# Down projections that add the residual x late and load their weights first, and a first half step whose tokens all load at once

## The chip, the cores and the metric

The kernel runs on one core of one Trainium2 chip, in float32 with float32r matmul operands. The metric is the device time of one execution in microseconds (us), lower is better. The time of a kernel is the median of several executions; the profile shows one execution, with a time of its own.

The engines have short names throughout: PE is TensorE (matmuls), PEld its weight loads, DVE is VectorE, ACT is ScalarE, POOL is GpSimd, SP is SyncE, which here only issues DMA transfers. ACT issues DMA transfers too (ACTq rows), in the same in-order queue as its computing instructions.

## The reference, cut to what matters

One layer of a streaming encoder. 1024 prompt tokens and 8 x 16 sample tokens (together 1152 tokens, nine tiles of 128) go through two SwiGLU half steps around a mixer:

```python
def _swiglu(x, w_gate, w_up, w_down):
    return (jax.nn.silu(x @ w_gate) * (x @ w_up)) @ w_down

x = x + 0.5 * _swiglu(_rms_norm(x, norm_ff1), w_ff1_gate, w_ff1_up, w_ff1_down)
h = _rms_norm(x, norm_mix); proj = h @ w_in
# RWKV-7 scan on one part of proj, chunk-band attention (with a bias table) on the rest
x = x + concat(rwkv_out, att) @ w_out
x = x + 0.5 * _swiglu(_rms_norm(x, norm_ff2), w_ff2_gate, w_ff2_up, w_ff2_down)
y = _rms_norm(x, norm_final)
```

D_MODEL is 1024 and D_FF 2816. The change touches only the two half steps and the making of the attention bias tables, which is spread through the first down projection.

## The kernel before, in words

**Precision.** Every float32 matmul operand is split into a float32r high part (an ACT copy) and a low part (a subtraction on POOL or DVE); a product is three matmuls: high by high, high by low, low by high.

**Half step, first stage (gate and up).** The tokens are held in two parts (640 and 512 tokens). Each part is normed, transposed on PE and turned into seven "forms", sums and differences of quarter blocks for a seven-product block scheme: three in a tile FX (tag F3) and four in FT (tag F4). `_x_forms` makes them, one of four column chunks c at a time: transposes (L251), copies and splits (L261, L262), differences (L263), the ACT copy of FT (L269) and its low parts (L271 on DVE, L272 on POOL). `_w_forms` loads a 1 MB weight block into a `raw` tile and yields its seven forms (`frm` tiles, seven buffers; combinations in `cmb`, L297). `_gate_up` runs blocks m = 0 to 10: seven products t for either part p, gate, then up, and writes the hidden block to DRAM (`hd`, `he`). In block 0 of the first half step the order of products is set by `k.lead`: the first part's first three products, then the rest.

At the start of the kernel five tiles of tokens load, then a second norm loop loads four more into the same seven `frm` buffers that the weight forms use; it is written between the making and the running of part 0's form generator.

**Half step, second stage (`_down`).** Eleven blocks m of two hidden rows of 128. For each block the hidden values `hr` (1.1 MB) are read back and split into `h` (L431 on ACT, L432 on POOL), and two weight rows `raw` (0.5 MB each) are read and split into `spl` (L162 on ACT, L163 on POOL). Then for nine token tiles and two column halves, six matmuls (L449 to L451) fill one PSUM bank (eight banks rotate), and DVE adds it to x (L453). In block 0 the nine x tiles are loaded beside it (L423). In the last block each x tile is handed on (`done`): to the norm of the mixer in the first half step, to the final norm and the output in the second.

**Beside the first down projection** `_bias_tables` runs as a generator, one step per block from block 1 on: vectors, then a small table, then for each of four head pairs a row broadcast, a skewed copy through DRAM, 12 transfers in all, a few DVE operations and a write. Its transfers are all on ACT's queue, each waiting for the one before.

**What sets the order.** The framework does not keep each engine's program order. It runs the program through its own cost model and gives every engine and DMA queue, at each moment of that model, the earliest-written instruction that is ready; the order found there is then fixed, and on the chip each queue runs it strictly in order, waiting at its head. So an instruction written late can stand early in its queue if the model found it ready, and the model's idea of a transfer's length decides it. Memory follows the same rule: pools lie on a left and a right stack, and a tile of a new pool waits for the tiles that lay there before.

Of the kernel before, what the change touches and what calls it, by code (L numbers as in the profile page):

```python
# [9 lines left out]
F32 = mybir.dt.float32  # L10
# [10 lines left out]
NT = 9  # L21
# [90 lines left out]
def _bias_tables(k, a):  # L112

    nc = k.nc
    _more_vectors(k, a)
    yield
    room = k.xgp.tile([P, KC * TG], F32, tag="xg", bufs=6, name="room")
    tab = room[:8, 0:257]  # L120
    nc.scalar.dma_start(tab, a["rel_bias"][0])
    ext = room[:8, 384:768]
    nc.gpsimd.memset(ext, 0.0)
    nc.vector.tensor_scalar(ext[:, 127:384], tab, tab[:, 0:1], None, ALU.subtract)
    extd = k.tc.dram_tile([8, 384], F32, name="ext_d")
    nc.scalar.dma_start(extd, ext)
    k.maskb = room[:, 768:768 + P].rearrange("p (b q) -> p b q", q=NQ)
    nc.gpsimd.memset(k.maskb, 0.0)
    for step, base in ((-1, 0), (1, NQ - 1)):
        nc.gpsimd.affine_select(  # L130
            out=k.maskb, in_=k.maskb, pattern=[[step * NQ, NB], [0, NQ]], compare_op=ALU.is_ge,
            fill=NEG, base=base, channel_multiplier=-step)
    for p in range(NPAIR):
        yield
        buf = k.xgp.tile([P, KC * TG], F32, tag="xg", bufs=6, name="bias")
        rows = buf[:, 0:768]
        near = buf[:, 768:1280].rearrange("p (h c) -> p h c", h=2)
        samp = buf[:, 1280:1792].rearrange("p (h c) -> p h c", h=2)
        new = buf[:, 1792:1792 + 288].rearrange("p (h c) -> p h c", h=2)
        nc.scalar.dma_start(  # L140
            rows, extd[2 * p:2 * p + 2].rearrange("h c -> (h c)")[None, :].to_broadcast([P, 768]))
        sk = k.tc.dram_tile([P, 768], F32, name=f"skew{p}")
        nc.scalar.dma_start(sk, rows)

        nc.scalar.dma_start(near, bass.AP(sk.tensor, sk.offset + 127, [[767, P], [384, 2], [1, 256]]))
        for b in range(NB):
            nc.scalar.dma_start(new[b * NQ:(b + 1) * NQ],
                                bass.AP(sk.tensor, sk.offset + 127, [[767, NQ], [384, 2], [1, 144]]))
        nc.vector.memset(near[0:64, :, 192:256], NEG)
        for h in range(2):  # L150
            nc.vector.tensor_copy(samp[:, h, 0:P], new[:, h, 0:P])
            nc.vector.tensor_tensor(
                samp[:, h, P:].rearrange("p (b q) -> p b q", q=NQ),
                new[:, h, None, P:P + NQ].to_broadcast([P, NB, NQ]), k.maskb, ALU.add)
        k.bias[p] = k.tc.dram_tile([P, 4, 256], F32, name=f"bias{p}")
        nc.scalar.dma_start(k.bias[p].rearrange("p h c -> p (h c)"), buf[:, 768:1792])
# [8 lines left out]

def _load_w(k, src, shape, rearr, **kw):

    raw = k.w.tile([P] + shape, F32, tag="raw", bufs=k.nraw, name="raw")
    k.wq.dma_start(raw, src.rearrange(rearr, **kw) if rearr else src)
    pool, nspl = k.spl  # L170
    d = pool.tile([P, 2] + shape, F32R, tag="spl", bufs=nspl, name="spl")
    _split(k, d, raw)
    return d
# [6 lines left out]
def _rms(k, x, junk):  # L180

    nc = k.nc
    ss = k.sm.tile([P, 1], F32, tag="ss", name="ss")
    rs = k.sm.tile([P, 1], F32, tag="rs", name="rs")
    nc.scalar.activation(junk, x, AF.Square, accum_out=ss)
    nc.vector.tensor_scalar(rs, ss, 1.0 / DM, 1e-5, ALU.mult, ALU.add)
    nc.gpsimd.tensor_tensor(ss, rs, k.mhalf[:, 0:1], ALU.pow)
    return ss
# [87 lines left out]
def _form_tile(pool, part, forms):  # L276
    return pool.tile([P, 2, forms, 4, PARTS[part][1]], F32R, tag=f"F{forms}", bufs=1, name="F")
# [30 lines left out]
    yield form(a22), 6, "a"  # L308


def _gate_up(k, wg, wu, hd, m, between=None):

    nc = k.nc
    hs = [k.hx.tile([P, 2, 2, n], F32, tag=f"hs{p}", bufs=1, name="hs") for p, (o, n) in enumerate(PARTS)]
    for up, w in enumerate((wg, wu)):
        source = _w_forms(k, w[:, 2 * m * P:2 * m * P + 2 * P])
        forms = [] if m == 0 and not up else list(source)
        state = [{}, {}]
        turns = [(t, p) for t in range(7) for p in range(2)]
        if m == 0 or (up and m == NF // 2 - 1):  # L320
# [78 lines left out]
def _down_w(k, wd, f):  # L399
    raw = k.w.tile([P, DM], F32, tag="raw", bufs=k.nraw, name="raw")  # L400
    k.nc.sync.dma_start(raw, wd[f * P:(f + 1) * P, :])
    pool, n = k.dspl[f % len(k.dspl)]
    d = pool.tile([P, 2, DM], F32R, tag="spl", bufs=n, name="spl")
    _split(k, d, raw)
    return d


def _down(k, s, pool, wd, hd, xd, done, beside=(), then=None):

    nc = k.nc  # L410
    mm = nc.tensor.matmul
    beside = iter(beside)
    k.hp = hp = [pool(s, "ha")]
    k.h = hp[0]
    if len(k.dspl) == 1:
        k.dspl.append((pool(s, "wb"), 2))
    hp.append(pool(s, "hb"))
    k.xp = pool(s, "xb")
    k.psum, k.ptag, k.pbufs = pool(s, "psum_b", space=PSUM), "g", 8

    def x_load(i):
        k.x.append(k.xp.tile([P, DM], F32, tag=f"x{i}", bufs=1, name="x"))
        nc.sync.dma_start(k.x[i], xd[i])  # L423

    k.x = []
    for m in range(NF // 2):
        raw = hp[0].tile([P, 2, T], F32, tag="hr", bufs=1, name="hr")
        nc.sync.dma_start(raw, hd[m])
        h = hp[m % 2].tile([P, 2, 2, T], F32R, tag="h", bufs=1, name="h")
        for f in range(2):  # L430
            nc.scalar.activation(h[:, 0, f], raw[:, f], AF.Copy)  # L431
            nc.gpsimd.tensor_tensor(h[:, 1, f], raw[:, f], h[:, 0, f].bitcast(F32), ALU.subtract)  # L432
        d = [_down_w(k, wd, f) for f in (2 * m, 2 * m + 1)]
        if m == 0:
            for i in range(2):
                x_load(i)
        if m:
            next(beside, None)
        if m == NF // 2 - 1 and then is not None:
            then()  # L440
        for i in range(NT):
            if m == 0 and i + 2 < NT:
                x_load(i + 2)
            a = slice(i * P, (i + 1) * P)
            for n in range(2):
                b = slice(512 * n, 512 * n + 512)
                ps = _bank(k, "pd")
                for f in range(2):
                    mm(ps, h[:, 0, f, a], d[f][:, 0, b], start=f == 0, stop=False)  # L449
                    mm(ps, h[:, 0, f, a], d[f][:, 1, b], start=False, stop=False)  # L450
                    mm(ps, h[:, 1, f, a], d[f][:, 0, b], start=False, stop=f == 1)  # L451
                xs = k.x[i][:, b]
                nc.vector.tensor_tensor(xs, ps, xs, ALU.add)  # L453
            if m == NF // 2 - 1:
                done(i)

# [815 lines left out]
def tile_encoder_step(ctx: ExitStack, tc: tile.TileContext, *aps):  # L1272
# [4 lines left out]
    k = _K()  # L1277
    k.nc, k.tc, k.o, k.dq, k.wq, k.aq = nc, tc, o, nc.sync, nc.sync, nc.scalar
    k.qd, k.kd, k.qs, k.bias = {}, {}, {}, {}
    k.nraw, k.nspl, k.nt, k.nu = 2, 4, 20, 7  # L1280

    def pool(stack, name, side="left", **kw):
        kw.setdefault("bufs", 1)
# [2 lines left out]
    def x_rows(i):  # L1286
        return a["x_prompt"][0, i * P:(i + 1) * P, :] if i < NPT else a["x_sample"].rearrange("b t d -> (b t) d")
# [20 lines left out]
    with ExitStack() as s_rw, ExitStack() as s_xg:  # L1308
# [3 lines left out]
        with ExitStack() as sr, ExitStack() as s:  # L1312
            k.F = [(_form_tile(pool(sr, "fx", "right"), 0, 3), _form_tile(pool(s, "ft"), 0, 4))]
            f1 = pool(s, "f1")
            k.F.append((_form_tile(f1, 1, 3), _form_tile(f1, 1, 4)))
            k.ny, k.nyb = 4 * PARTS[0][1], 3
            k.hx = pool(s, "hx")
            k.w = pool(s, "wa")
            k.bsp, k.bst, k.nbs, k.bsw = k.hx, "y", 3, k.ny
            k.lead = 3  # L1320
            _gate_up_banks(k, s, pool)
            _constants(k, a)
            gain = _gain(k, a["norm_ff1"][0], k.hx, "hs1")

            def norm_part(p):
                xns = []
                for i in (range(5), range(5, 9))[p]:
                    x = k.w.tile([P, DM], F32, tag="frm", bufs=7, name="xn")
                    nc.sync.dma_start(x, x_rows(i))
                    junk = k.hx.tile([P, 4 * 320], F32, tag="hs0", bufs=1, name="junk")  # L1330
                    rs = _rms(k, x, junk[:, :DM])
                    nc.vector.scalar_tensor_tensor(x, x, rs, gain, ALU.mult, ALU.mult)
                    xns.append(x)
                return xns

            xns = norm_part(0)
            part = _x_forms(k, 0, xns)
            xns = norm_part(1)
            for _ in part:
                pass  # L1340
            for m in range(NF // 2):
                _gate_up(k, w[0], w[1], hd, m, lambda: [None for _ in _x_forms(k, 1, xns)])
        k.w = pool(s_xg, "w2", "right")
        k.nraw, k.spl = 2, (k.w, 3)
        k.dspl = [k.spl]
# [180 lines left out]
```

## Time and profile before

| | |
|---|---|
| time of before, median of 3 runs | 2612.99 us (2608.03 to 12799.39) |
| the profiled execution: its own time | 2605.25 us |
| its span, first to last instruction | 2603.5 us |
| mean granted TensorE clock | 0.962 |
| PE busy | 2422.6 us, 93% |
| DVE, ACT, POOL busy | 1124.8, 899.8, 1076.5 us |
| DMA | 284.75 MB, mean 109 GB/s |

Between the span and the profiled execution's own time lie 1.75 us. A row of a timeline gives the start in us from the span's start, the busy time in us of the merged instructions, engine, line of the code, operation, output and inputs, shapes, count, and in brackets the idle time of the engine before it with what ended it. The granted clock is a share of full speed: 1.00 is 2.4 GHz and 0.50 is 1.2 GHz.

The stages of the half steps in this execution: start and first gate/up stage 0 to 575 us, first down projection 575 to 882, second gate/up stage up to 2311, second down projection from there to the end.

### The profile page before, as it was taken

To read this page: it belongs to the slowest core of one execution; us is meant where nothing else is said; L and a number is where in the kernel's file an instruction comes from. 1 tells how busy PE (TensorE), PEld (TensorE's weight loads), DVE (VectorE), ACT (ScalarE), POOL (GpSimd) and SP (SyncE) were. 2 spreads that over 40 slices of the span, in tenths; PEclk is the share of its full clock that TensorE was granted. 3 is DMA by queue.
4 is the path that set the end of the run, shared out by engine and by line. 5 is a ranking of instruction groups with operands and counts; after the bars stand their busy time and mean duration, and the time that the engine had idled before them with its cause. 6 is when DMAs were issued, how large, how long until landed. Compare 5 with 4: busy or idle time off the path is not lost.

```text
span 2603.5 us, 43481 instructions
## 1 busy us (share of the span) xinstructions
PE 2422.6 (93%) x17415; PEld 2161.5 (83%) x17415; DVE 1124.8 (43%) x2346; ACT 899.8 (35%) x1903; POOL 1076.5 (41%) x966
## 2 busy tenths in 40 slices
PE   4999999988999999999997999897999999989998
PEld 3899999986888799899874666676999999988886
DVE  6322222214544533856854666346222222225555
ACT  5333333321111443443323576524333333321112
POOL 4545454444433233443213443105554544544332
PEclk8999999999999999999996899998999999999999
DMA  3222112227322324543658994522221122252221
GB/s 113 67 68 86 56 63 86 67 83 269 113 77 70 107 63 133 168 132 104 190 148 197 219 206 112 175 91 65 67 86 57 62 86 68 69 197 102 77 102 73
DMA packets 230283, 284.75 MB, mean 109 GB/s; under 512 B 54920, under 2 KB 183552, under 8 KB 227264
## 3 DMA queue, kind: packets, MB, share of 16 engines
q1 hardware_dynamic: 194044, 226.72, 27.8%
q0 software_dynamic: 7648, 25.43, 4.1%
q10 hardware_dynamic: 28388, 29.81, 3.5%
q8 instruction: 137, 2.24, 0.4%
q14 instruction: 66, 0.54, 0.1%
HBM read 191.79 MB, written 90.12 MB: 108 GB/s over the span
## 4 chain that ended last, share of the span: by engine, by line
PE 42%; DVE 5%; POOL 3%; issue 3%; ACT 2%; DMA 2%; ACTq 0%; POOLq 0%; DVEq 0%
PE pa L341 3%; PE pd L450 3%; PE pd L451 3%; PE pd L449 3%; PE pa L343 3%; PE pa L342 3%; PE pb L341 2%; PE pb L342 2%; PE pb L343 2%; POOL frm L292 2%; PE ps_s L1132 1%; PE ps_o L1186 1%; PE ps_pt L1171 1%; PE ps_yc L975 1%; PE ps_wo L1261 1%
## 5 line engine op out<-in xcount | busy, mean ns | idle before, releaser
L341 PE MATMUL pa<-F,frm 128*128 128x256 f32 (+1 forms) x1408 | 424.6, 302 | 34.7 <-ACT r L348 25.2
L343 PE MATMUL pa<-F,frm 128*128 128x256 f32 (+1 forms) x1408 | 419.3, 298 | 2.7 <-POOL frm L292 2.7
L342 PE MATMUL pa<-F,frm 128*128 128x256 f32 (+1 forms) x1408 | 419.3, 298 | 2.1 <-POOL F L272 2.1
L453 DVE TENSOR_TENSOR x<-pd,x 128x512 f32<-128x512 f32 x396 | 270.0, 690 | 243.1 <-PE pd L451 228.8
L163 POOL TENSOR_TENSOR spl<-raw,spl 128x1024 fp32r<-128x1024 f32 x78 | 187.6, 2408 | 453.0 <-ACT spl L162 453.0
L449 PE MATMUL pd<-spl,h 128*128 128x512 f32 x792 | 314.0, 397 | 14.8 <-ACT spl L162 12.1
L450 PE MATMUL pd<-spl,h 128*128 128x512 f32 x792 | 311.9, 394 | 13.3 <-POOL spl L163 13.3
L292 POOL TENSOR_TENSOR frm<-cmb,frm 128x512 fp32r<-128x512 f32 x176 | 230.1, 1309 | 221.7 <-ACT frm L291 221.3
L343 PE MATMUL pb<-F,frm 128*128 128x320 f32 (+1 forms) x1056 | 312.7, 296 | 3.1 <-POOL frm L292 3.1
L342 PE MATMUL pb<-F,frm 128*128 128x320 f32 (+1 forms) x1056 | 312.2, 296 | 3.1 <-DVE F L271 3.1
L341 PE MATMUL pb<-F,frm 128*128 128x320 f32 (+1 forms) x1056 | 313.3, 297 | 1.2 <-ACT frm L291 1.2
L451 PE MATMUL pd<-spl,h 128*128 128x512 f32 x792 | 311.8, 394 | 0.0
L341 PEld LDWEIGHTS pa<-F,frm 128*128 128x128 f32 x1408 | 268.9, 191 | 44.4 <-ACT r L348 33.0
L343 PEld LDWEIGHTS pa<-F,frm 128*128 128x128 f32 x1408 | 269.1, 191 | 3.5 <-POOL frm L292 3.5
L342 PEld LDWEIGHTS pa<-F,frm 128*128 128x128 f32 x1408 | 269.4, 191 | 2.5 <-POOL F L272 2.5
L292 POOL TENSOR_TENSOR frm<-raw,frm 128x512 fp32r<-128x512 f32 x132 | 173.8, 1318 | 186.7 <-ACT frm L291 186.7
L162 ACT ACTIVATE spl<-raw 128x1024 fp32r<-128x1024 f32 x78 | 82.2, 1055 | 406.3 <-PE pd L451 342.7
L343 PEld LDWEIGHTS pb<-F,frm 128*128 128x128 f32 x1056 | 200.2, 190 | 3.8 <-POOL frm L292 3.8
L342 PEld LDWEIGHTS pb<-F,frm 128*128 128x128 f32 x1056 | 200.1, 190 | 3.3 <-DVE F L271 3.3
L341 PEld LDWEIGHTS pb<-F,frm 128*128 128x128 f32 x1056 | 200.0, 189 | 1.8 <-ACT frm L291 1.8
L449 PEld LDWEIGHTS pd<-spl,h 128*128 128x128 f32 x792 | 150.1, 190 | 48.5 <-ACT spl L162 12.3
L450 PEld LDWEIGHTS pd<-spl,h 128*128 128x128 f32 x792 | 150.1, 189 | 48.3 <-POOL spl L163 16.2
(259 smaller groups left out, 4572.7 us busy)
## 6 DMA issues: line engine op xcount, KB each, us to landing
raw<-in_w_ff_gate_dram SPq DMA_DIRECT2D x22, 1024.0 KB
raw<-in_w_ff_up_dram SPq DMA_DIRECT2D x22, 1024.0 KB
raw<-in_w_ff_down_dram SPq DMA_DIRECT2D x44, 512.0 KB
raw<-in_w_in_dram SPq DMA_DIRECT2D x26, 512.0 KB
hr<-hd SPq DMA_DIRECT2D x11, 1152.0 KB
hr<-he SPq DMA_DIRECT2D x11, 1152.0 KB
q<-qk POOLq DMA_DIRECT2D x24, 384.0 KB, 7.6
x<-xd SPq DMA_DIRECT2D x18, 512.0 KB
```

Of the source, the lines that this page charges most:

```text
L162: k.nc.scalar.activation(dst[:, 0], raw, AF.Copy)
L163: k.nc.gpsimd.tensor_tensor(dst[:, 1], raw, dst[:, 0].bitcast(F32), ALU.subtract)
L292: nc.gpsimd.tensor_tensor(d[:, 1], x, d[:, 0].bitcast(F32), ALU.subtract)
L341: nc.tensor.matmul(ps, frm[:, 0, c], F[:, 0, jj, c], start=new and c == 0, stop=False, **kw)
L342: nc.tensor.matmul(ps, frm[:, 0, c], F[:, 1, jj, c], start=False, stop=False, **kw)
L343: nc.tensor.matmul(ps, frm[:, 1, c], F[:, 0, jj, c], start=False, stop=c == 3, **kw)
L449: mm(ps, h[:, 0, f, a], d[f][:, 0, b], start=f == 0, stop=False)
L450: mm(ps, h[:, 0, f, a], d[f][:, 1, b], start=False, stop=False)
L451: mm(ps, h[:, 1, f, a], d[f][:, 0, b], start=False, stop=f == 1)
L453: nc.vector.tensor_tensor(xs, ps, xs, ALU.add)
L975: mm(py[s, hh % 2], wout[:, hh, L:], mov[:, hh], start=True, stop=True)
L1132: mm(ps, q.qs[i // 3][:, j, h, t:t + P], q.ks[h][:, c0:c0 + n], start=j == 0, stop=j == 1)
```

## The change

Four edits.

1. `_down` writes a block's two weight loads and splits ahead of its hidden load and split; in block 0 the low part of h is subtracted on DVE instead of POOL.
2. `_down` no longer loads x in block 0. There ACT copies the bank into the x tile; from block 1 to 9 one tile of x per block is loaded into a single buffer `xin` and added to its x tile by DVE (128x1024), written after the first token tile.
3. `_bias_tables` yields more often, and a step is taken at the fourth and the seventh token tile of each block from 1 on, instead of once ahead of the block.
4. The first half step loads token tiles 0 to 4 into a spare tile (`hold`, where part 1's F3 tile comes later), the first gate weights, then tiles 5 to 8 into two `frm` buffers and one `raw` buffer, instead of waiting for `frm` buffers; the first weight form is written ahead of the token forms, part 0's forms ahead of the second norms, and `k.lead` is 5 instead of 3. (`_load_w` is adapted to a wider `raw` tile, without another transfer.)

```diff
@@ _bias_tables
         for h in range(2):
+            yield
             nc.vector.tensor_copy(samp[:, h, 0:P], new[:, h, 0:P])
@@ _gate_up
-def _gate_up(k, wg, wu, hd, m, between=None):
+def _gate_up(k, wg, wu, hd, m, between=None, gates=None, lead=()):
-        source = _w_forms(k, w[:, 2 * m * P:2 * m * P + 2 * P])
-        forms = [] if m == 0 and not up else list(source)
+        source = gates if gates and not up else _w_forms(k, w[:, 2 * m * P:2 * m * P + 2 * P])
+        forms = list(lead) if m == 0 and not up else list(source)
@@ _down
-    def x_load(i):
-        k.x.append(k.xp.tile([P, DM], F32, tag=f"x{i}", bufs=1, name="x"))
-        nc.sync.dma_start(k.x[i], xd[i])
-
-    k.x = []
+    k.x = [k.xp.tile([P, DM], F32, tag=f"x{i}", bufs=1, name="x") for i in range(NT)]
     for m in range(NF // 2):
+        d = [_down_w(k, wd, f) for f in (2 * m, 2 * m + 1)]
         raw = hp[0].tile([P, 2, T], F32, tag="hr", bufs=1, name="hr")
         nc.sync.dma_start(raw, hd[m])
         h = hp[m % 2].tile([P, 2, 2, T], F32R, tag="h", bufs=1, name="h")
         for f in range(2):
             nc.scalar.activation(h[:, 0, f], raw[:, f], AF.Copy)
-            nc.gpsimd.tensor_tensor(h[:, 1, f], raw[:, f], h[:, 0, f].bitcast(F32), ALU.subtract)
-        d = [_down_w(k, wd, f) for f in (2 * m, 2 * m + 1)]
-        if m == 0:
-            for i in range(2):
-                x_load(i)
-        if m:
-            next(beside, None)
+            (nc.gpsimd if m else nc.vector).tensor_tensor(
+                h[:, 1, f], raw[:, f], h[:, 0, f].bitcast(F32), ALU.subtract)
+        if 1 <= m <= NT:
+            xin = k.xp.tile([P, DM], F32, tag="xin", bufs=1, name="xin")
+            nc.sync.dma_start(xin, xd[m - 1])
...
         for i in range(NT):
-            if m == 0 and i + 2 < NT:
-                x_load(i + 2)
+            if i == 1 and 1 <= m <= NT:
+                nc.vector.tensor_tensor(k.x[m - 1], k.x[m - 1], xin, ALU.add)
+            if m and i in (3, 6):
+                next(beside, None)
...
                 xs = k.x[i][:, b]
-                nc.vector.tensor_tensor(xs, ps, xs, ALU.add)
+                if m:
+                    nc.vector.tensor_tensor(xs, ps, xs, ALU.add)
+                else:
+                    nc.scalar.copy(xs, ps)
@@ tile_encoder_step, first half step
-            k.F.append((_form_tile(f1, 1, 3), _form_tile(f1, 1, 4)))
-            k.lead = 3
+            k.lead, k.raww = 5, 2 * DM
...
-            xns = norm_part(0)
-            part = _x_forms(k, 0, xns)
-            xns = norm_part(1)
-            for _ in part:
+            hold = f1.tile([P, 2 * 3 * 4 * PARTS[1][1]], F32, tag="F3", bufs=1, name="hold")
+            xns = [normed(i, hold[:, i * DM:(i + 1) * DM]) for i in range(5)]
+            gates = _w_forms(k, w[0][:, 0:2 * P])
+            lead = [next(gates)]
+            for _ in _x_forms(k, 0, xns):
                 pass
-            for m in range(NF // 2):
-                _gate_up(k, w[0], w[1], hd, m, lambda: [None for _ in _x_forms(k, 1, xns)])
+            rest = [k.w.tile([P, DM], F32, tag="frm", bufs=7, name="xn") for _ in range(2)]
+            two = k.w.tile([P, 2 * DM], F32, tag="raw", bufs=2, name="xn")
+            rest += [two[:, :DM], two[:, DM:]]
+            xns = [normed(5 + i, x) for i, x in enumerate(rest)]
+            k.F.append((_form_tile(f1, 1, 3), _form_tile(f1, 1, 4)))
+            _gate_up(k, w[0], w[1], hd, 0, lambda: [None for _ in _x_forms(k, 1, xns)], gates, lead)
+            for m in range(1, NF // 2):
+                _gate_up(k, w[0], w[1], hd, m)
+            k.raww = DM
```

`normed(i, x)` is the body of the old norm loop for one tile: load, square and sum on ACT (L185), 1/rms (L186, L187), scale on DVE (L1332).

## Rows read from the trace of the kernel before

**Rows 1.** Busy time by stretches of 20 us: for PE, PEld, DVE, ACT and POOL the busy us and the count, then granted clock, DMA share, GB/s.

```profile
40.00:60.00 20.00, 11.17 (x51) 8.93 (x52) 15.56 (x32) 9.06 (x20) 9.00 (x6) 0.72 0.00 1
60.00:80.00 20.00, 15.02 (x83) 14.15 (x83) 11.19 (x18) 10.36 (x19) 15.99 (x11) 0.77 0.17 52
580.00:600.00 20.00, 7.80 (x20) 5.29 (x21) 3.64 (x4) 4.22 (x4) 9.95 (x5) 0.54 0.87 329
620.00:640.00 20.00, 16.64 (x71) 12.60 (x70) 14.17 (x23) 6.35 (x6) 14.92 (x6) 1.00 0.67 223
660.00:680.00 20.00, 20.00 (x88) 16.28 (x87) 10.51 (x16) 4.12 (x4) 10.27 (x5) 1.00 0.33 118
2300.00:2320.00 20.00, 13.24 (x97) 12.11 (x96) 2.20 (x6) 5.38 (x7) 12.84 (x8) 0.88 0.67 228
```

**Rows 2.** Timeline of SP's DMA queue in the first gate/up stage: the token loads, and the writes of hidden blocks 1 and 2 (two transfers each).

```profile
0.81 3.77 SPq L1329 DMA_DIRECT2D xn<-in_x_prompt_dram  x7
29.68 0.34 SPq L1329 DMA_DIRECT2D xn<-in_x_prompt_dram  x1
...
159.12 1.18 SPq L377 DMA_DIRECT2D hd<-hs  x2
205.65 1.24 SPq L377 DMA_DIRECT2D hd<-hs  x2
```

**Rows 3.** Timelines of DVE and POOL in the first 75 us, put in order of time: differences of part 0 (L263, 128x320), the norm of token tile 7 (L1332), and the low parts of FT (L272; 128x960 is part 0, 128x768 part 1).

```profile
32.23 1.28 DVE L263 TENSOR_TENSOR bs<-ps_n,bs 128x320 f32<-128x320 f32 x3
36.10 2.25 POOL L272 TENSOR_TENSOR F<-bs,F 128x960 fp32r<-128x960 f32 x1
36.18 3.26 DVE L1332 SCALAR_TENSOR_TENSOR xn<-xn,ss,gain 128x1024 f32<-128x1024 f32 x1 [0.94 <-POOL ss L187]
41.83 0.88 DVE L263 TENSOR_TENSOR bs<-ps_n,bs 128x320 f32<-128x320 f32 x2
72.11 1.98 POOL L272 TENSOR_TENSOR F<-bs,F 128x768 fp32r<-128x768 f32 x1
```

**Rows 4.** What PE waited for from 575 to 900 us, the first down projection: us in total, times, longest.

```profile
PE pd L449 <- ACT spl L162: 12.1, 1, 12.1
PE pd L450 <- POOL spl L163: 6.5, 3, 4.4
...
PE pd L449 <- DVE x L453: 2.0, 2, 1.7
```

**Rows 5.** Timeline of SP's queue at the start of the first down projection, and of SP's waits from 560 to 660 us.

```profile
564.66 13.67 SPq L428 DMA_DIRECT2D hr<-hd  x2
578.43 0.86 SPq L401 DMA_DIRECT2D raw<-in_w_ff_down_dram  x2
579.38 24.60 SPq L423 DMA_DIRECT2D x<-in_x_prompt_dram  x8
...
611.82 0.80 SPq L401 DMA_DIRECT2D raw<-in_w_ff_down_dram  x2
...
SPq L401 <- DMA bias<-skew: 21.2, 4, 10.6
```

**Rows 6.** Timelines of PE, ACT, POOL and DVE at the start of the first down projection.

```profile
595.07 0.79 PE L450 MATMUL pd<-spl,h 128*128 128x512 f32 x1 [0.67 <-POOL spl L163]
...
583.90 2.22 ACT L431 ACTIVATE h<-hr 128x1152 fp32r<-128x1152 f32 x2 [10.90 <-DMA hr<-hd]
586.02 1.04 ACT L162 ACTIVATE spl<-raw 128x1024 fp32r<-128x1024 f32 x1
590.85 1.06 ACT L162 ACTIVATE spl<-raw 128x1024 fp32r<-128x1024 f32 x1 [3.79 <-DVE room L124]
615.54 1.06 ACT L162 ACTIVATE spl<-raw 128x1024 fp32r<-128x1024 f32 x1 [23.64 <-DMA raw<-in_w_ff_down_dram]
...
585.14 5.20 POOL L432 TENSOR_TENSOR h<-hr,h 128x1152 fp32r<-128x1152 f32 x2 [5.07 <-ACT h L431]
590.31 4.71 POOL L163 TENSOR_TENSOR spl<-raw,spl 128x1024 fp32r<-128x1024 f32 x2
```

**Rows 7.** Timelines of PE, ACT and POOL at the start of the second down projection.

```profile
2310.79 0.39 PE L449 MATMUL pd<-spl,h 128*128 128x512 f32 x1
2316.59 0.79 PE L450 MATMUL pd<-spl,h 128*128 128x512 f32 x1 [5.41 <-POOL spl L163]
2319.59 0.80 PE L450 MATMUL pd<-spl,h 128*128 128x512 f32 x1 [1.35 <-POOL spl L163]
2325.68 0.40 PE L449 MATMUL pd<-spl,h 128*128 128x512 f32 x1
...
2311.26 1.06 ACT L162 ACTIVATE spl<-raw 128x1024 fp32r<-128x1024 f32 x1 [1.02 <-DMA raw<-in_w_ff_down_dram]
...
2308.31 5.25 POOL L432 TENSOR_TENSOR h<-hr,h 128x1152 fp32r<-128x1152 f32 x2 [0.18 <-ACT h L431]
2314.21 2.33 POOL L163 TENSOR_TENSOR spl<-raw,spl 128x1024 fp32r<-128x1024 f32 x1
2317.19 2.34 POOL L163 TENSOR_TENSOR spl<-raw,spl 128x1024 fp32r<-128x1024 f32 x1
```

**Rows 8.** An ACT copy out of PSUM, and the steady pace of the down stage: an eviction on DVE with the wait for PE ahead of it.

```profile
566.32 0.39 ACT L348 ACTIVATE r<-pa 128x256 f32<-128x256 f32 x1 [8.18 <-PE pa L343]
...
2355.84 0.69 DVE L453 TENSOR_TENSOR x<-pd,x 128x512 f32<-128x512 f32 x1 [0.67 <-PE pd L451]
```

More of the change, by code (lines that the diff above doesn't have):

```diff
@@ L166, in _load_w @@
 def _load_w(k, src, shape, rearr, **kw):
-    raw = k.w.tile([P] + shape, F32, tag="raw", bufs=k.nraw, name="raw")
+    raw = k.w.tile([P, k.raww], F32, tag="raw", bufs=k.nraw, name="raw")[:, :DM]
+    if len(shape) == 2:
+        raw = raw.rearrange("p (a b) -> p a b", b=shape[1])
     k.wq.dma_start(raw, src.rearrange(rearr, **kw) if rearr else src)
@@ L1279, in tile_encoder_step @@
     k.qd, k.kd, k.qs, k.bias = {}, {}, {}, {}
-    k.nraw, k.nspl, k.nt, k.nu = 2, 4, 20, 7
+    k.nraw, k.raww, k.nspl, k.nt, k.nu = 2, DM, 4, 20, 7
     def pool(stack, name, side="left", **kw):
@@ L1323, in tile_encoder_step, with normed @@
             gain = _gain(k, a["norm_ff1"][0], k.hx, "hs1")
[L1325 to L1334, printed above, removed]
-            xns = norm_part(0)
-            part = _x_forms(k, 0, xns)
-            xns = norm_part(1)
-            for _ in part:
-                pass
-            for m in range(NF // 2):
-                _gate_up(k, w[0], w[1], hd, m, lambda: [None for _ in _x_forms(k, 1, xns)])
+            def normed(i, x):
+                nc.sync.dma_start(x, x_rows(i))
+                junk = k.hx.tile([P, 4 * 320], F32, tag="hs0", bufs=1, name="junk")
+                rs = _rms(k, x, junk[:, :DM])
+                nc.vector.scalar_tensor_tensor(x, x, rs, gain, ALU.mult, ALU.mult)
+                return x
+            hold = f1.tile([P, 2 * 3 * 4 * PARTS[1][1]], F32, tag="F3", bufs=1, name="hold")
[3 more added lines that the diff above has]
+            for _ in _x_forms(k, 0, xns):
+                pass
+            rest = [k.w.tile([P, DM], F32, tag="frm", bufs=7, name="xn") for _ in range(2)]
[7 more added lines that the diff above has]
+            k.raww = DM
         k.w = pool(s_xg, "w2", "right")
```

## The prediction, made before the changed kernel ran

> **What bounds the kernel now.** I read the busy time by stretches first, because it tells stages apart: in the steady part of a down projection PE is busy for 20.00 of 20 us at full clock, while at 40 to 80 us, 580 to 600 us and 2300 to 2320 us it is not, and the granted clock is down there as well, 0.54 in the lowest [rows 1]. So PE is the bound of the half steps, DVE, ACT and POOL have room there (10.5, 4.1 and 10.3 of 20 us), and only the three places where a stage begins can give time back. The middle of the kernel, between the two half steps, is not touched. Then I read what PE waited for and, in the timelines, what had made the releaser late.
>
> *The start.* Seven token tiles load at once, two more wait for `frm` buffers until 29.68 us [rows 2]. The norm of tile 7 then takes DVE at 36.18, ahead of the last differences of part 0: chunk 2 of four has them done at 33.5 (32.23 + 1.28), chunk 3 only at 42.7. Part 1's last low part is done at 74.1 (72.11 + 1.98) [rows 3]. Hidden blocks are written every 46.5 us (205.65 - 159.12), so block 0 ended about 46.5 us before 159.1, at 112.6: 38.5 us after the last form [rows 2, 3].
>
> *The first down projection.* PE waits 12.1 us for the first weight split, then three times for POOL's low parts, in all 6.5 us, and 2.0 us for evictions [rows 4]. Why the weights are late is in SP's queue: the weights of block 0 left at 578.43, behind the hidden load of block 1, which had to wait until POOL had read the buffer; eight x loads follow until 604, the ninth behind them, and the weights of block 1 leave only at 611.82, after waits for bias-table transfers of ACT's queue (21.2 us in four) [rows 5]. On POOL the low parts of block 1's h (585.14 to 590.34) stand ahead of block 0's weights (590.31 to 595.02), and ACT held the second weight for 3.79 us behind a bias-table step. PE runs without gaps from 595.07 [rows 6].
>
> *The second down projection.* PE waits 5.41 and 1.35 us for POOL, which does 5.25 us of h and then 2 x 2.33 us of weights; PE runs on from 2319.59, at half clock (matmuls of 0.8 us) until 2325.68, where they take 0.40 us [rows 7].
>
> **The change, part by part.**
>
> *Start.* Nine token tiles and 1 MB of gate weights now go out first, the up weights later. At the 329 GB/s of 580 to 600 us [rows 1] these 5.8 MB take 18 us, so all tokens should be there by about 20 us. DVE's work is the same too; what goes is its order. Without the norm of tiles 7 and 8 between chunks 2 and 3, chunk 3 follows chunk 2 by one chunk's DVE work, about 4 us (eight operations of around 0.47 us, from 0.88 for two and 1.28 for three [rows 3]): 37.5 instead of 42.7, 5 us. The norms of tiles 5 and 6, loaded with the first seven, stood ahead of part 0's forms and now stand behind: 2.5 us more. I carry 7.5 us through to part 1's last form, because DVE idles 4.4 and 8.8 us of the two stretches from 40 to 80 [rows 1] and can take the norms in. With five products instead of three run ahead of part 1, two products of part 0 move into time that was a wait: a product is 1/14 of a block's part-0 half, 46.5 x 320/576 / 14 = 1.8 us, so 3.5 us. Sum **-11 us**. Ends: -18 (DVE idles 13.2 us from 40 to 80, and all of it goes, with the 3.5 us), and +3 for the first weight form, which now stands ahead of the token forms on ACT: if its 1 MB lands late, ACT waits for it, and 1 MB at that rate, 3.2 us, is the price.
>
> *First down projection.* Written first does not mean issued first: the old program too had block 0's weights ahead of block 1's hidden load, and the queue has them the other way round [rows 5]. So I do not count on weights that arrive before PE needs them. What frees the queue is that the hidden buffer is read by DVE: 1152 elements at the pace of the 1.28 us norm of 1024 [rows 3] are 1.44 us against POOL's 2.6 (5.20 for two [rows 6]), so the weights leave some 3.5 us earlier, near 575; the first landed 7.6 us after issue (586.02 - 578.43), the rest of the chain is as before. PE runs on from about 591: -4. The x loads leave the queue, so block 1's weights can leave earlier; of the 3.4 us that block 1 cost PE (1.4 of the 6.5 and the 2.0 [rows 4]) I take back 2, since waits on ACT's transfers remain. ACT's evictions: a copy of 256 columns is 0.39 us and one of 1024 is 1.06, so 512 take 0.6 [rows 6, 8]; 18 of them, 11 us, lie beside PE's 18 x 1.36 = 24.5 us [rows 8]: nothing, as long as ACT isn't held for longer than eight banks cover, 10.9 us. The nine additions of `xin`, 1.28 us each and 3.26 at worst beside POOL [rows 3], fall on a DVE that is half idle: nothing; without that cover 11.5 us a down projection. The load of one tile per block has 24.5 us of time; the DVE addition that waits for it has the evictions of its block queued behind it, and PE behind those after eight banks. The later steps of the bias tables are needed only far behind, in attention. Sum **-6 us**; ends -21 (the 12.1, 6.5 and 2.0 all go) and +13 (second rival).
>
> *Second down projection.* POOL loses the 5.25 us of h. The second weight's split on ACT ends at 2312.3, its low part 2.33 us later, with one 0.7 us product of the stage before between: about 2315.4 instead of 2319.6, so -4.2. A rule about DVE and POOL takes part of it back. The norm of 36.18 that took 3.26 us ended 1.1 us after POOL's operation beside it (36.10 + 2.25 = 38.35; 39.44), just its own 1.28 us: the two did not run side by side [rows 3]. The two subtractions of 1.44 us on DVE may so hold POOL for up to 2.9 us; I take 1.2. The Trainium skill, page "SBUF — State Buffer", section "Who interferes with whom", says that a DVE instruction with two SBUF inputs and a GpSimd instruction that reads SBUF exclude each other for their whole length; this trace agrees, and by that rule alone the term would be -1.3 instead of -4.2. The clock: 14 matmuls run at half pace from 2319.59 to 2325.68, 6.1 us instead of 3.2 (1.36/6 each). The waits of 1.4 and 1.7 us in block 1 lie in 620 to 640 us, where the clock is 1.00 [rows 1, 4]; after the wait of 5.41 it was half [rows 7]. The new wait lies between; I take half of 2.9. Sum **-4.5 us**; ends -1 and -11 (5.4 + 1.4 + 2.9, and more than that isn't lost). The nine x loads ahead of the first evictions cost PE nothing there before.
>
> Sum -21.5 us on the profiled execution's own 2605.25 (its span is 2603.5): 2583.8. The lowest run shown is 2.8 above that execution, the median 7.7, with an outlier that lifts it; I add 2.8: **2586 us**, 1% below 2612.99. About 2%, 52 us, is what a measurement of this kernel can tell from no change.
>
> **The rivals.**
>
> *Weights in time.* The queue's order does change, weights go out while the last products still run, and PE passes from one stage to the next without its wait and without half clock. Against it: the old order [rows 5]; for it: the second down projection, where weights followed the hidden load at once. Price: -15, -21 and -11, so 2605.25 + 2.8 - 47 = 2561.
>
> *ACT holds the evictions (slower).* ACT waited 23.64 us for a weight of block 1 [rows 6], whose load waited for bias-table transfers that ACT itself issues. Before, nothing that PE needed at once stood behind; now block 0's evictions do. Eight banks cover 10.9 us; a wait of 23.6 costs 12.7. With one such wait the first down projection loses 12.7 instead of gaining 6, and the time is 2605. With one for either weight of the block it loses 25.4 against 15.5 gained elsewhere: 2618, slower than before. It decides from holds of 26.4 us together beyond the cover of the first. Against it: the x loads that made transfers slow are gone.
>
> *The order doesn't change.* The framework's model leaves the forms of the start and the queue of the first down projection nearly as they are, and only POOL's relief counts: -3, -3.5 and -3, so 2598.
>
> **How the numbers follow.** Forecast 0.50; order unchanged 0.20; weights in time 0.13; ACT holds once 0.10, twice 0.07. The range of 8 in 10 goes from 2561 to 2606: it leaves out the slower case and the better half of the best one, and some of each end. Faster by over 2% (below 2560.7) needs nearly all of the first rival's sum: 0.07. Slower by over 2% has no case here, I leave 0.02 for one I don't see. Within 2%: 0.91.
>
> **What would show it.** Right: part 1's last L272 ends near 66 instead of 74; block 1's hidden write stands some 11 us earlier; the first weight of the down projection leaves SP near 575 and PE is gapless from about 591 after the old stage end; at the second, PE's wait for POOL's weights is about 2 us and few matmuls take 0.8 us. Wrong: an ACT wait over 11 us in block 0 with PE waiting for ACT's copies; DVE waiting for `xin`; or a weight load issued before the last gate/up product, which makes it the first rival.

## The result, and the profile after

The changed kernel takes 2578.59 us, median of four runs (2576.16 to 2579.73), against 2611.04 us for the kernel before, median of four of which one is the outlier of 12799.39. The ratio of the means, without that outlier, is 0.9878, with a 95% interval from 0.9859 to 0.9898: 1.2% faster, clear of noise, though less than the 2% that the prediction took as the least one could tell. The forecast was 2586 us. The profiled execution has a span of 2578.0 us, 25.5 us less than before, where the sum of the terms had been 21.5. (The medians are 32.5 us apart because the profiled execution of the kernel before, 2605.25 us, was a quick one.)

The total was near; its terms were not. I cut each profiled execution at five places: the write of hidden block 1, the end of the last gate/up matmul, the start of the first down projection's last matmul, the end of the second gate/up stage, and the end of the span. The first column runs from the span's start to the first mark and each of the next four from one mark to the next, in us; "middle" is everything between the two down projections, which no kernel here edits.

| kernel | to block 1's write | to the end of gate/up | first down | middle | second down | span |
|---|---|---|---|---|---|---|
| before | 159.1 | 415.9 | 306.7 | 1429.3 | 292.6 | 2603.5 |
| after | 154.4 | 416.6 | 291.1 | 1430.1 | 285.7 | 2578.0 |
| e1 start only | 155.9 | 416.1 | 307.9 | 1430.6 | 291.7 | 2602.3 |
| e2 order only | 159.4 | 416.0 | 306.1 | 1432.7 | 289.7 | 2603.9 |
| e3 DVE low part only | 158.7 | 416.6 | 307.6 | 1432.6 | 288.6 | 2604.1 |
| e4 late x only | 159.3 | 416.1 | 305.0 | 1430.4 | 293.1 | 2603.9 |
| e5 DVE low part and late x | 161.2 | 416.7 | 296.9 | 1424.5 | 288.0 | 2587.2 |
| e6 after, old written order | 153.9 | 416.6 | 293.1 | 1433.2 | 289.4 | 2586.2 |
| e7 after, POOL low part | 155.9 | 415.9 | 302.8 | 1431.8 | 290.4 | 2596.8 |
| e8 after, early x | 156.0 | 416.8 | 309.3 | 1428.3 | 286.9 | 2597.3 |
| e9 after, old steps | 154.5 | 416.5 | 291.5 | 1430.6 | 285.0 | 2578.1 |
| e10 after, lead 3 | 150.2 | 416.4 | 290.1 | 1429.7 | 285.2 | 2571.6 |
| e11 after, FT on DVE | 152.8 | 416.9 | 290.3 | 1432.1 | 284.6 | 2576.8 |
| e12 both of these | 147.0 | 416.8 | 290.0 | 1434.7 | 285.0 | 2573.5 |

The middle says how far a single execution can be read: it spreads over 10 us. In e6 PE, ACT and DVE run it in the same order as in the changed kernel, and it is 3.1 us longer. Nine executions of the kernel before, beside e12, lie between 2603.48 and 2617.88. So I compare stages and what ended the waits in them, not single totals.

From before to after, rounded from hundredths: start -4.7, gate/up +0.8, first down -15.6, middle +0.9, second down -6.8.

By stretches of 20 us (PE, PEld, DVE, ACT, POOL busy and counts, then granted clock, DMA share, GB/s), answering [rows 1]:

```profile
40.00:60.00 20.00, 13.88 (x66) 11.12 (x66) 11.97 (x24) 9.11 (x21) 8.59 (x7) 0.76 0.01 2
60.00:80.00 20.00, 17.25 (x106) 16.07 (x106) 14.39 (x24) 10.08 (x20) 16.24 (x11) 0.78 0.33 106
580.00:600.00 20.00, 20.00 (x79) 16.08 (x79) 0.00 (x0) 11.59 (x18) 12.41 (x5) 0.89 0.64 223
2280.00:2300.00 20.00, 18.18 (x124) 16.35 (x124) 5.48 (x8) 8.94 (x12) 14.11 (x9) 1.00 0.78 257
```

From 580 to 600 us PE is now busy throughout, where it was busy for 7.80 us. What PE waited for from 555 to 900 us (us in total, times, longest), answering [rows 4]:

```profile
PE pd L449 <- ACT spl L163: 2.6, 1, 2.6
PE pd L450 <- POOL spl L164: 2.5, 2, 1.5
PE pa L344 <- DVE y L357: 0.8, 1, 0.8
```

And from 2270 us to the end, answering [rows 7]:

```profile
PE pd L451 <- DVE h L432: 1.3, 2, 0.7
PE pd L449 <- ACT h L431: 0.5, 1, 0.5
```

The 12.1, 6.5 and 2.0 us of the first down projection became 2.6, 2.5 and nothing; the 6.8 us of the second became 1.8. The reason stands in SP's queue, answering [rows 2, 5]:

```profile
154.41 1.18 SPq L380 DMA_DIRECT2D hd<-hs  x2
...
559.96 0.34 SPq L428 DMA_DIRECT2D hr<-hd  x1
568.21 0.82 SPq L404 DMA_DIRECT2D raw<-in_w_ff_down_dram  x2
571.37 0.33 SPq L428 DMA_DIRECT2D hr<-hd  x1
576.04 2.94 SPq L404 DMA_DIRECT2D raw<-in_w_ff_down_dram  x2
```

One of SP's waits there, from 555 to 660 us:

```profile
SPq L404 <- DMA vrows<-in_mu_shift_dram: 7.8, 1, 7.8
```

Block 0's weights now leave ahead of block 1's hidden load, 2.9 us before the gate/up stage ends (571.06), and block 1's at 576.04 instead of 611.82.

### The profile page after: what moved, and what is told of

It reads as the page before. It is cut to its first block, busy times and chain, and to the rows that moved or that the text cites. A ratio compares the mean times of both kernels' runs of the same rounds, so it can differ in the third digit from the quotient of the medians.

```text
span 2578.0 us, 43273 instructions
## 1 busy us (share of the span) xinstructions
PE 2421.8 (94%) x17415; PEld 2160.3 (84%) x17415; DVE 1127.8 (44%) x2332; ACT 918.4 (36%) x1939; POOL 1077.6 (42%) x962
## 4 chain that ended last, share of the span: by engine, by line
PE 73%; DVE 8%; POOL 5%; issue 5%; ACT 3%; DMA 3%; ACTq 0%; POOLq 0%; DVEq 0%; SPq 0%
PE pd L449 7%; PE pd L451 7%; PE pd L450 7%; PE pa L344 7%; PE pa L346 6%; PE pa L345 6%; PE pb L344 3%; PE pb L345 3%; PE pb L346 3%; POOL frm L295 3%; PE ps_p L229 2%; PE ps_p L230 2%; PE ps_p L231 2%; PE ps_s L1135 2%; PE ps_pt L1174 1%
## 5 line engine op out<-in xcount | busy, mean ns | idle before, releaser
L454 DVE TENSOR_TENSOR x<-pd,x 128x512 f32<-128x512 f32 x360 | 244.1, 688 | 201.8 <-PE pd L451 201.8
L294 ACT ACTIVATE frm<-cmb 128x512 fp32r<-128x512 f32 x176 | 110.3, 628 | 198.7 <-PE pa L346 121.5
L451 PEld LDWEIGHTS pd<-spl,h 128*128 128x128 f32 x792 | 149.4, 189 | 36.3 <-DVE h L432 2.2
```

What stands on the lines that cost most here:

```text
L294: nc.scalar.activation(d[:, 0], x, AF.Copy)
```

## The experiments

Each ran once with a profile, unless a number of runs is given.

**One part at a time, on the kernel before.** e1 takes the start alone (edit 4), e2 to e4 take one edit of `_down` each:

```diff
e2: the line  d = [_down_w(k, wd, f) ...]  moves ahead of the hidden load
e3: +  (nc.gpsimd if m else nc.vector).tensor_tensor(h[:, 1, f], ...)
e4: ACT evicts block 0, one xin per block from 1 on, no x loads in block 0
```

> The kernel before with the start edit alone (tokens at once, first weight form early, lead 5). The trace of the changed kernel writes hidden block 1 at 154.41 us instead of 159.12, and everything else it gains lies later. If the start edit stands by itself, this kernel writes block 1 near 154.4, the rest is as before, and the total is 4 to 6 us under before. If the start gained more and gave it back to the rest of the change, or the other way round, block 1 comes before 152 or after 157.

> The kernel before with only the written order changed: a block's weight loads ahead of its hidden load, the low part of h still on POOL. Theory A (the order in which the loads are written does not decide the queue; the engine of the low part does): in the first down projection block 1's hidden load still stands ahead of block 0's weights in SP's queue, PE's first wait there stays near 12 us and PE runs gapless some 20 us after the last gate/up product, as before; total within 4 us of before. Theory B (weights written first is what brought the 15 us): the weights leave before block 1's hidden load, the wait falls to about 3 us, total 8 us or more under before.

> The kernel before with only the low part of block 0's h moved from POOL to DVE in both down projections. Theory A: block 1's hidden load has to wait longer in the framework's model, so block 0's weights go out ahead of it; PE's first wait falls from 12.1 to 3 to 5 us, PE runs gapless 8 to 12 us earlier in the first down projection, and the second one gains 3 to 5 us; total 12 to 16 us under before. Theory B: only POOL's relief, 4 us and 3 us, total 5 to 8 us under before.

> The kernel before with only x late: no x loads in block 0, ACT copies the banks there, one tile of x per block after that; written order, POOL's low part and the steps of the bias tables as before. Theory A: block 0 starts as late as before (wait near 12 us), and only the 3.4 us that block 1 cost PE go; total 2 to 5 us under before. Theory C (the x loads crowded the transfers, so that weights were late): the first waits fall by 6 us or more, total 8 us or more under before. If ACT's bias-table waits hold the evictions, PE waits for ACT's copies and the total is over before.

Measured: 2604.01, 2605.61, 2605.85 and 2605.66 us, against 2604.07 for the kernel before. No part alone gains anything in total, where 4 to 6 us were expected of e1, 12 to 16 (or 5 to 8) of e3 and 2 to 5 of e4. In the stages, e1 gains 3.2 us at the start. e2 leaves the first down projection as it was, with the weights behind both hidden loads (theory A), and takes 2.9 us off the second. e3 does move the weights ahead of block 1's hidden load, and PE's first wait falls to 2.6 us, as its theory A had it, yet the stage ends no earlier. SP's queue in e2, then in e3:

```profile
564.97 13.38 SPq L429 DMA_DIRECT2D hr<-hd  x2
578.44 0.86 SPq L401 DMA_DIRECT2D raw<-in_w_ff_down_dram  x2
```

```profile
572.45 0.82 SPq L401 DMA_DIRECT2D raw<-in_w_ff_down_dram  x2
575.63 0.33 SPq L428 DMA_DIRECT2D hr<-hd  x1
```

e4 leaves the queue as before (weights at 579.01, first wait 12.4 us) and takes 1.7 us off.

**Two parts together, on the kernel before.** e5 is e3 and e4 in one.

> The kernel before with two of the parts together: DVE subtracts the low part of block 0, and x is added late (ACT evicts block 0); the start, the written order of weights and hidden load, and the steps of the bias tables are those of before. Theory (neither part gains alone, because early weights need evictions that don't wait for x loads, and late x needs early weights): the weights leave SP before block 1's hidden load, near 570 us, the first down projection ends 12 to 15 us earlier than before (near 868), the second one gains 5 to 7, so 18 to 21 us off, 2583 to 2587. Rival (the parts add up as they did alone, -1.3 and 0 at the first down projection and about -4 at the second): 2598 to 2604.

Measured: 2589.02 us against 2612.09. The first down projection falls by 9.8 us, less than expected, where e3 and e4 alone gave +0.9 and -1.7: the two parts need each other. PE still lost 4.2 us to evictions (the copies of finished PSUM banks) on DVE, which stood behind slow bias-table operations (2.18 us at 644.36 and 2.76 at 646.46) of the kind that e8 shows below. Why this build meets them and the changed kernel does not isn't settled: putting the old steps into the changed kernel doesn't bring them (e9), the old written order brings back 1.6 us of such a wait (e6).

**One part taken out of the changed kernel.** The kernel before took 2612.09 us beside e6 to e8 and 2608.05 (median of seven) beside e9.

```diff
e6: the line  d = [_down_w(k, wd, f) ...]  back behind the hidden load and split
e7: -  (nc.gpsimd if m else nc.vector).tensor_tensor(h[:, 1, f], ...)   +  nc.gpsimd.tensor_tensor(...)
e8: nine x loads in block 0, DVE adds every bank to x, no xin
e9: _bias_tables and its steps as before
```

> The changed kernel, but each block's hidden load is again written ahead of its two weights. Theory (the queue's order comes from when the hidden buffer is free, not from the written order): SP issues the weights of block 0 ahead of block 1's hidden load all the same, every stage mark within 2 us of the changed kernel, time 2577 to 2583. Rival (the written order moves the weights): they leave some 8 us later, near 576, and the time is 2587 or more.

> The changed kernel, but POOL subtracts the low part of block 0 as before. Theory: block 1's hidden load waits for POOL and is again ahead of the weights, which leave near 575; the first down projection ends 12 to 15 us later than in the changed kernel; the second waits for POOL some 5 us longer and falls to half clock; 2596 to 2601. Rival (late x carries the first down projection and POOL only its own 2.6 us per subtraction): 3 us in the first and 4 in the second, 2587.

> The changed kernel, but the nine x tiles are loaded in block 0 and DVE adds each bank to x, as before. Theory (with the weights early, evictions wait for x loads that stand behind other transfers): PE waits in the first block for DVE's evictions, together with later weights of block 1 some 13 us, first down projection ends near 876 instead of 862, 2590 to 2595; second down projection within 2 us of the changed kernel. Rival (the x loads are hidden, only the weights' place counts): within 3 us, 2577 to 2583.

> The changed kernel with the old steps of the bias tables: one step ahead of each block from 1 on, instead of at its fourth and seventh token tile. Theory (a step written ahead of the block stands ahead of block 1's evictions on DVE, which wait behind its transfers, as in the run of the two parts on the kernel before, where PE lost 4.2 us to them): the first down projection, from the end of the gate/up stage to its last matmul, takes 294 to 297 us instead of 291.1, the other stages are unchanged, 2581 to 2586. Rival (the steps are off the path): 290 to 292.5 us.

*e7* (2598.49 us) is as the theory had it. SP's queue has block 1's hidden load first again, and PE's waits are close to those of before. SP's timeline in e7:

```profile
561.48 14.13 SPq L428 DMA_DIRECT2D hr<-hd  x2
575.71 0.86 SPq L404 DMA_DIRECT2D raw<-in_w_ff_down_dram  x2
```

PE's waits in e7 from 555 to 900 us:

```profile
PE pd L449 <- ACT spl L163: 12.5, 1, 12.5
PE pd L450 <- POOL spl L164: 5.1, 2, 4.4
```

The first down projection is 11.7 us longer than in the changed kernel (12 to 15 were expected), the second 4.7. So in the first down projection the queue's order hangs on the engine that reads the hidden buffer, not on the written order: e6 keeps the weights in front with the old written order.

*e6* (2587.86 us) nevertheless misses its 2577 to 2583, at the other end. The first down projection is only 2.0 us longer, but the second 3.7. There SP's queue does follow the written order; in the changed kernel, and then in e6:

```profile
2280.74 0.82 SPq L404 DMA_DIRECT2D raw<-in_w_ff_down_dram  x2
2282.50 0.33 SPq L428 DMA_DIRECT2D hr<-he  x1
```

```profile
2286.21 0.34 SPq L427 DMA_DIRECT2D hr<-he  x1
2286.61 12.96 SPq L404 DMA_DIRECT2D raw<-in_w_ff_down_dram  x3
```

In e6 PE waits 3.6 us for POOL's weights and then runs 13 matmuls at half clock; in the changed kernel the weights are split before the stage begins and none runs at half clock. 3.1 us more of e6's total lie in the middle, which it doesn't touch.

*e8* (2599.04 us) loses even more of the first down projection than expected, 18.2 us, but not by the mechanism I had named. No eviction is seen to wait for an x load. The largest wait of PE ends at 657.41 us:

```profile
657.41 0.79 PE L447 MATMUL pd<-spl,h 128*128 128x512 f32 x1 [6.82 <-DVE x L451]
```

DVE in e8 just before it:

```profile
647.02 2.15 DVE L152 COPY bias<-bias 128x128 f32<-128x128 f32 x1 [0.79 <-DMA bias<-skew]
649.09 2.48 DVE L153 TENSOR_TENSOR bias<-bias,room 128x128 f32<-128x128 f32 x1
651.50 2.63 DVE L152 COPY bias<-bias 128x128 f32<-128x128 f32 x1
654.04 2.71 DVE L153 TENSOR_TENSOR bias<-bias,room 128x128 f32<-128x128 f32 x1
656.68 5.46 DVE L451 TENSOR_TENSOR x<-pd,x 128x512 f32<-128x512 f32 x9
```

And POOL in e8 at that time:

```profile
646.67 4.75 POOL L164 TENSOR_TENSOR spl<-raw,spl 128x1024 fp32r<-128x1024 f32 x2 [16.57 <-ACT spl L163]
651.39 5.22 POOL L432 TENSOR_TENSOR h<-hr,h 128x1152 fp32r<-128x1152 f32 x2
```

The same kind of step in the changed kernel:

```profile
647.85 0.23 DVE L152 COPY bias<-bias 128x128 f32<-128x128 f32 x1 [4.85 <-DMA bias<-skew]
647.99 0.28 DVE L153 TENSOR_TENSOR bias<-bias,room 128x128 f32<-128x128 f32 x1
```

Four small operations of a bias-table step, 1.0 us together when POOL is idle, took 10.0 us beside POOL's splits, each about as long as one POOL operation. Nine evictions stood behind them, and PE behind those. e3 shows the same at 649.75 to 659.46 (2.11, 2.77, 2.62 and 2.44 us, and 6.35 us of PE). The rest of e8's loss lies at block 1, whose weights left at 602.04 behind nine x loads: 5.9 us more waits for ACT and POOL (6.5 + 4.5 against 2.5 + 2.6), and about 20 more matmuls at half pace, some 0.2 us each. So early x costs twice: its loads push block 1's weights back, and splits on POOL fall onto DVE's bias steps. That the second follows from the first wasn't tried apart, nor was the loading of x apart from the evictions on DVE, which e8 brings back with it.

*e9* (2579.91 us) fits the rival: 291.5 us, no wait for evictions. The new steps are worth nothing measurable.

**The start.** Two edits of the changed kernel, then both:

```diff
e10: k.lead = 3 instead of 5
e11: +  (nc.vector if part == 0 and c > 1 else nc.gpsimd).tensor_tensor(FT[:, 1, 1:4, c], ...)
e12: both
```

> The changed kernel with three products ahead of part 1 instead of five. Theory (part 1's forms come when they come, and products of part 0 fill the time before): the forms of part 1 at the same place, block 1's hidden write 3 to 4 us later, 157.4 to 158.4 instead of 154.41, all behind it shifted. Rival (the lead only changes which wait shows): 153.5 to 155.5.

> The changed kernel, but the low parts of FT for chunks 2 and 3 of part 0 are subtracted on DVE instead of POOL. Theory (the norms of tiles 5 to 8 took 6.11 and 3.49 us for two beside POOL's 5.36 us for two of these, where 1.28 each was expected; the exclusion ate the gain of the new order): the norms go back to about 1.3 us each, DVE gains about 7 us and pays about 2.5 for the subtractions, part 1's forms and block 1's hidden write come 2 to 4 us earlier, 150.5 to 152.5, and the time falls by as much. Rival (DVE is the chain either way, and what it takes over stands ahead of the norms): block 1's write within 1 us of 154.41 or later, no gain.

> The changed kernel with both edits of the two runs before: three products ahead of part 1, and the low parts of FT for chunks 2 and 3 of part 0 on DVE. Theory (both shorten the same chain at different places, norms on DVE and part 1's transposes behind products on PE, so they add): block 1's hidden write at 154.41 - 4.2 - 1.6 = 148.6 (148 to 149.5), everything behind unchanged, median 2570 to 2574. Rival (one hides the other): 150.2 and 2573 or later.

*e10* (2573.31 us) contradicts my theory outright: with two products fewer ahead of part 1, block 1's write comes 4.2 us *earlier*. In the changed kernel PE runs products of part 0 from 47.33 to 53.8 us, and part 1's next transposes stand behind them, at 55.06; in e10 these transposes begin at 51.70. PE in the changed kernel, then in e10:

```profile
55.06 0.89 PE L254 MATMUL ps_n<-ident,xn 128*128 128x128 f32 x4 [1.27 <-ACT bs L267]
```

```profile
51.70 0.80 PE L254 MATMUL ps_n<-ident,xn 128*128 128x128 f32 x4
```

PE's queue accounts for 2.1 of these 3.4 us, up to 53.8. For the other 1.27 PE waits for ACT's copy `bs` of the transposes before (L267). The two additional products are the first whose results are finished, and their SiLU, with a 1.28 us table load, stands ahead of that copy in ACT's queue. ACT in the changed kernel, then in e10, where the table load comes at 62.50:

```profile
52.98 1.28 ACT L361 ACT_TABLE_LOAD   x1 [2.08 <-DVE y L357]
54.27 0.47 ACT L361 ACTIVATE hs<-y 128x320 f32<-128x320 f32 x1
54.65 0.36 ACT L267 ACTIVATE bs<-ps_n 128x256 f32<-128x256 f32 x1
```

```profile
47.63 0.38 ACT L267 ACTIVATE bs<-ps_n 128x256 f32<-128x256 f32 x1
```

In e10 the two products then run between part 1's transposes, from 52.25 to 58; in the changed kernel they are already done, PE is busy for 1.93 of the 4 us from 56 to 60, and the granted clock (the third figure from the end below) falls to 0.50 (1.2 GHz), while it stays at 1.00 in e10. By stretch, the changed kernel, then e10:

```profile
60.00:68.00 8.00, 6.30 (x25) 5.47 (x26) 4.42 (x13) 4.61 (x11) 4.24 (x4) 0.50 0.04 7
```

```profile
60.00:68.00 8.00, 6.04 (x44) 5.34 (x42) 4.79 (x9) 6.61 (x11) 6.41 (x4) 1.00 0.47 143
```

Part 1's last low part on POOL is done at 68.1 us (66.12 + 1.99) instead of 72.8 (70.72 + 2.04).

*e11* (2577.38 us median of four; ratio to before 0.9875, 0.9851 to 0.9898) moves the mark by 1.6 us, less than expected. The first two norms of the second group fall from 6.11 to 2.47 us, but the other two stay at 3.48. In the six builds whose start is that of the changed kernel (after, e1, e6 to e9) the mark lies between 153.9 and 156.0, so 152.8 is only just outside.

*e12* takes 2575.21 us (median of five, 2572.39 to 2576.57; ratio 0.9871, 0.9850 to 0.9891), outside the 2570 to 2574 that were expected. Block 1's write stands at 147.0, 7.5 us before the changed kernel's, more than the sum of the two; up to the end of the first down projection 8.4 us are kept. The middle of its profiled execution is 4.6 us longer, so the total gains 3.4 us on the changed kernel's median. The two ratios can't be told apart; that the start is shorter can.

## Why the prediction was right in the total and wrong in its terms

**Start, -11: measured -4.7.** The wrong step is "so 3.5 us" for the two products run ahead. The work that ends PE's wait, part 1's transposes and ACT's copies of them, stands behind these products on PE and behind their SiLU on ACT: the step cost 4.2 us (e10) instead of giving 3.5. The other term, 7.5 us for the order of norms and chunks, is about right: with lead 3 part 1's last form is done 6.0 us earlier than before (68.1 against 74.1) and block 1's write stands 8.9 us earlier. Of what lies behind the last form I had counted nothing; the granted clock from 72 to 80 us is 1.00 in e10 and was 0.57 before. DVE's norms in the changed kernel, answering [rows 3], show what I had left out:

```profile
33.11 6.11 DVE L1331 SCALAR_TENSOR_TENSOR xn<-xn,ss,gain 128x1024 f32<-128x1024 f32 x2
40.79 3.49 DVE L1331 SCALAR_TENSOR_TENSOR xn<-xn,ss,gain 128x1024 f32<-128x1024 f32 x2 [0.44 <-POOL ss L190]
```

POOL in the changed kernel, the same stretch and part 1's last low part:

```profile
32.78 5.36 POOL L275 TENSOR_TENSOR F<-bs,F 128x960 fp32r<-128x960 f32 x2
...
70.72 2.04 POOL L275 TENSOR_TENSOR F<-bs,F 128x768 fp32r<-128x768 f32 x1
```

Two norms beside POOL took 6.11 us, where 2 x 1.28 was expected. The sign named beforehand, an end of part 1's last low part near 66 us, isn't seen in the changed kernel (72.8); e10 comes near it (68.1) and e12 passes it (62.93 + 2.00 = 64.9).

**First down projection, -6: measured -15.6.** "Written first does not mean issued first" held for the written order (e2, e6). The conclusion, "I do not count on weights that arrive before PE needs them", failed: the edit that I had counted as 3.5 us less to wait in the queue (its own figures, two subtractions of 1.44 us instead of 2.6, give 2.3), the subtraction on DVE, turns the queue's order round and lets the weights leave at 568.21, before the last gate/up product. That was the sign of the rival "weights in time", and the queue did go that way (e3, e7). The first weight was split 4.3 us after its load left (572.52), where I had taken 7.6 for the landing alone. What PE kept is waits of 2.6 and 2.5 us, and 15 matmuls ran at half pace instead of 12. Of the 2.6, up to 0.9 us may be a matter of ACT's queue, where the split of the first weight stands behind the write of the last hidden block: by the signals of its landing in the trace the weight was there at 571.6.

ACT in the changed kernel:

```profile
571.96 0.52 ACTq L380 DMA_DIRECT2D hd<-hs  x1
572.52 1.06 ACT L163 ACTIVATE spl<-raw 128x1024 fp32r<-128x1024 f32 x1 [3.88 <-POOL room L128]
```

**x late: 2 us counted, and the rest hung on it.** I took 2 of the 3.4 us of block 1; all went. But without this edit the first down projection loses 18.2 us (e8). The evictions on ACT took 0.59 us each and held nobody, as forecast; the additions of `xin` took 2.83 and 1.23 us without a wait of PE. The rival "ACT holds the evictions" had the right danger, a bias-table step in front of evictions, on the wrong engine: it is DVE that holds them, in e3, e5 and e8.

**Second down projection, -4.5: measured -6.8.** PE's waits fell from 6.8 to 1.8 us and the half clock went altogether (16 matmuls at about 0.2 us, some 3 us); the stretch behind PE's last matmul is 1.3 us longer (2603.5 - 2590.70 against 2578.0 - 2563.88). I had given the written order nothing here; it is worth 3.7 us (e6). The hold of POOL by DVE, put at 1.2 us, cost PE nothing: POOL had split the weights before DVE's subtractions began. PE's 1.3 us for `h` are the price of the new order: the hidden load now leaves behind the weights, ACT waited 3.19 us for it (2291.53), and the subtractions themselves took 1.42 and 1.55 us. POOL, then DVE, in the changed kernel:

```profile
2286.79 4.75 POOL L164 TENSOR_TENSOR spl<-raw,spl 128x1024 fp32r<-128x1024 f32 x2 [4.50 <-ACT spl L163]
```

```profile
2292.73 1.42 DVE L432 TENSOR_TENSOR h<-hr,h 128x1152 fp32r<-128x1152 f32 x1
```

**The sum.** -21.5 forecast, -25.5 measured: the start fell short by 6.3, gate/up by 0.8 and the middle by 0.9, the first down projection gave 9.6 more and the second 2.3 more. That the total came so near is luck: errors of 8 and 12 us had opposite signs. The range, 2561 to 2606, would have held either alone. Two ends given beside the terms don't follow from the rows named with them: -18 for the start (13.2 + 3.5 is 16.7) and -11 for the second down projection (5.4 + 1.4 + 2.9 is 9.7); nothing else was worked out from them.

## What to carry to other kernels

Products that are pulled forward to fill a wait stand in the same queue as the work that ends the wait, and so does the handling of their results on another engine; count what they hold up. A part that gains nothing alone (e2 to e4) may be the condition of another's gain, so take parts out of the finished change as well as putting them in one by one. And ask of each subtraction which engine frees its source: in the first down projection that decided which load left first, in the second the order in the source text did.

## What the runs showed of the hardware

Small DVE operations of 0.22 to 0.28 us took 2.11 to 2.77 us beside POOL's subtractions (e3, e8), where one POOL operation took 2.4 to 2.6 us (e8): the loss goes by the length of the POOL operation, not by their own. The Trainium skill, page "SBUF — State Buffer", section "Who interferes with whom", says that DVE and GpSimd share a port pair under an exclusive lock, and that a DVE instruction with two SBUF inputs contends there with a GpSimd instruction that reads SBUF, as a copy can too. The rows of e3 and e8 agree.

A load in SP's queue waited 7.8 us for a transfer of ACT's queue that fills another tile (`vrows`), by the inferred releaser; before the change the like of it cost 21.2 us in four waits [rows 5]. In the trace both signal their landing on one semaphore (number 100): the last signal of the `vrows` transfer is at 568.14 us, and the load leaves at 568.21. No run gave each a semaphore of its own, so that this sharing is the tie is likely and not shown.
